# A two-layer trunk on one core: the head of the S5 gate product in two passes, the modulation columns after it, and the S5 parameters ahead of the scale

## The chip, the core and the metric

The kernel runs on one core of one Trainium2 chip. The time is device microseconds (us) of one execution. The kernel before took 1287.72 us in the median of three runs (1287.06 to 1287.97). One further execution was profiled: it took 1287.81 us, and all numbers of a trace are from it. Engines are named as the profile names them: PE does matmuls (PEld loads their weights), DVE and ACT the elementwise work, POOL is hardly used here, and SP issues nearly all DMAs.

## The reference

The input x is 512 tokens by 1024 channels, with one conditioning vector c. Two layers follow each other: an S5 state-space mixer with a gated ConvFFN, then a forgetting attention with a second ConvFFN. Every sub-layer normalizes x (RMS), multiplies by g·(1 + scale) and adds shift, where shift, scale and the gate of the residual are thirds of one product of silu(c) with a 1024x3072 matrix. The change touches the S5 mixer alone:

```
def s5_mixer(h, w_in, lam_re, lam_im, log_dt, b_re, b_im, c_re, c_im, d_skip, w_glu, w_out):
    u = h @ w_in
    ... # lb = exp(lam*dt) and k from it, per group and state
    ... # bu = (k*b) u per token;  state: hs_t = lb * hs_(t-1) + bu_t   (complex, 64 groups x 64 states)
    y = y + d_skip.astype(f32) * u.astype(f32)      # y = Re(c . hs)
    y = jax.nn.gelu(y)
    y = y * jax.nn.sigmoid(y @ w_glu.astype(f32))   # the gate product
    return (y @ w_out.astype(f32)).astype(h.dtype)
```

## The kernel before

Channels lie on the 128 partitions in KT = 8 tiles, the 512 tokens along the free side. A product of full precision is made of three matmuls per input tile k and output tile m, of 128x128 weights with 128x512 inputs: rounded weights by the rounded input (a_hi,w_hi), rounded weights by what rounding took from the input (a_lo,w_hi), and the rest of the weights by the rounded input (a_hi,w_lo). For each output tile, the 128x1024 weights come by DMA into `raw`, ACT rounds them into `w_hi` (L236), and DVE subtracts into `w_lo` (L237). `w_hi` and `w_lo` have five buffers each, `raw` three, and product sums lie in four PSUM buffers (`mmp`); smaller sums share four others (`aux`).

**The start.** After the statistics of the norm, a chain of eleven small DVE instructions makes the reciprocal root (`rms_rows`, L347 to L357), interleaved with work of the S5 parameters (`s_turn`). A product of c with the scale third (`ada_pe`, L176, which leaves rows) is turned into columns on the partitions by matmuls with a selector (L132, L137); DVE makes `ga` of it (the norm's g times 1 + scale, L142) and multiplies it into the normalized x (`a_x`, L923, eight tiles). PE then makes the first tile of u = h @ w_in (L934), with the shift third between (L176). Each output tile of u is written by ACT, sent to DRAM, and read back in another layout. The generator `s5_params` computes lb, its powers and k on DVE in small tiles; it yields y of the norm's statistics, and then runs on behind the scale.

**The loop.** Each of eight passes m over 128 channels (eight groups) makes the tables of pass m+1 (DVE and PE: L738, L747, L758, L774; ACT copies them out, L781 and L785), a triangular table `kt` that goes through DRAM and comes back as `tw`, of which ACT makes `t` (L798), an input tile m+2 (L964), and steps of the modulation products (`ada`, L176): the gate third of this mixer at m = 0 and 1, the first two thirds of the next sub-layer after that. Then comes the scan of pass m (`s5_scan`): 32 matmuls of u into the states (L813), rotation on DVE (L824 to L827), the scan itself with factors `cf` that ACT makes (L830, scan L835), and the rotation back (L842 to L845), which ends with `ua`. The outputs of pass m are summed from 16 matmuls L855 (u by t) and 32 matmuls L863 (`ua` by the table w2), ACT applies the gelu (L869, `yg`), and the result goes to DRAM and back (`s_yd`, then `yt`, in y's layout). ACT and DVE split it into `a_hi` and `a_lo` (L981, L982; `parts`), the inputs of the gate product.

**The head of the gate product.** Four output tiles of the gate product (HEAD = 4, the four `mmp` buffers) are summed input tile by input tile, as y comes in: `glu_head(k)` makes the three matmuls of each of four tiles for input tile k (L253), 96 in all. The weights of a tile are loaded and split when it is first used. ACT then makes the sigmoid (L1031, from a table that it loads first), and the other four output tiles follow as an ordinary product (L253, 96 matmuls), and the output product (192) behind it.

**What sets the order.** In the start, the order on each engine is that of the code. In the loop, a recording layer of the kernel collects the instructions and places them by dependencies and estimated costs; a note such as `issue_after(ins)` or `behind(...)` holds an instruction behind another in that order. `HEAD`, the buffers' counts and the point at which a piece of code is reached thus set where it lands. PE, DVE, ACT and SP each run their instructions in the order in which they stand, and wait there.

## Time and profile before

| | us |
|---|---|
| median of three runs | 1287.72 |
| profiled execution | 1287.81 |
| its span on the core | 1286.0 |
| PE busy in the span | 1256.1 |
| DVE busy | 773.0 |
| ACT busy | 509.3 |
| first matmul of the first tile of u (L934) | at 24.82 |
| first matmul of the last-but-one scan (L813) | at 153.09 |
| first matmul of the gate product's other tiles (L253) | at 205.30 |

Times within the trace are counted from the span's start; the profiled execution is 1.8 us longer than its span, which is what lies around it. A row of the timeline gives start, duration, engine, line, operation, output<-inputs, shapes and count, and in brackets how long the engine idled before it, with what ended that. Durations of matmul rows overlap slightly, since matmuls are pipelined; the chain of waits counts each stretch of time once. PEclk (or the column after POOL in a table of windows) is the clock that TensorE was granted, 1.00 being full speed.

### The profile page before, as it was taken

How to read it: one execution, taken by the hardware profiler on the slowest of the kernel's cores; microseconds unless marked ns; L12 is line 12 of the kernel's file. 1: busy time of each engine (PE TensorE's matmuls, PEld its weight loads, DVE VectorE, ACT ScalarE, POOL GpSimd, SP SyncE). 2: the span in 40 equal slices, each digit the busy share in tenths (PEclk: the TensorE clock that was granted, in tenths of full speed). 3: DMA queues.
4: the chain of work that ended last, by engine and by line, in shares of the span. 5: the costliest groups of instructions: out<-in, count | busy, mean ns of one | idle time of the engine just before them, and what ended most of it. 6: DMA issues, size and time to landing. Idle time of an engine off the chain costs nothing.

```text
span 1286.0 us, 17721 instructions
## 1 busy us (share of the span) xinstructions
PE 1256.1 (98%) x6822; PEld 1011.8 (79%) x6822; DVE 773.0 (60%) x1398; ACT 509.3 (40%) x929; POOL 56.9 (4%) x103
## 2 busy tenths in 40 slices
PE   7999979999999999999999999999999999999997
PEld 2566667898877878788899878778988888888887
DVE  6899866578765546665466576655754433444443
ACT  2544445335332223333333466553543322333331
POOL 0000000000000000000000343230000000000000
PEclk9999969999999999999999999999999999999999
DMA  9777665337644746644404433323143234332221
GB/s 369 236 246 234 196 227 172 99 100 244 218 151 132 237 134 200 207 133 134 150 12 131 158 124 98 128 70 95 55 131 93 68 90 127 98 99 82 68 80 67
DMA packets 73060, 183.13 MB, mean 142 GB/s; under 512 B 23079, under 2 KB 25471, under 8 KB 71951
## 3 DMA queue, kind: packets, MB, share of 16 engines
q1 hardware_dynamic: 72687, 181.46, 44.4%
q8 instruction: 54, 0.88, 0.3%
q10 hardware_dynamic: 288, 0.52, 0.1%
q14 instruction: 31, 0.25, 0.1%
HBM read 175.04 MB, written 6.92 MB: 141 GB/s over the span
## 4 chain that ended last, share of the span: by engine, by line
PE 86%; DVE 5%; ACT 5%; DMA 2%; issue 2%; SPq 0%; DVEq 0%; ACTq 0%
PE mmp L253 68%; PE mmp L964 4%; PE mmp L1106 3%; ACT s L1217 2%; PE aux L1248 2%; PE aux L774 2%; PE mmp L176 1%; DVE w_lo L237 1%; PE aux L855 1%; PE aux L863 1%; PE aux L1231 1%; ACT w_hi L236 1%; DMA raw<-in_ada_w 1%; DMA raw<-in_w_up 1%; PE aux L137 1%
## 5 line engine op out<-in xcount | busy, mean ns | idle before, releaser
L253 PE MATMUL mmp<-a_hi,w_hi 128*128 128x512 f32 (+1 forms) x944 | 361.2, 385 | 2.5 <-ACT w_hi L236 1.3
L253 PE MATMUL mmp<-a_lo,w_hi 128*128 128x512 f32 (+1 forms) x944 | 358.7, 381 | 0.0
L253 PE MATMUL mmp<-a_hi,w_lo 128*128 128x512 f32 (+1 forms) x944 | 358.6, 381 | 0.0
L236 ACT ACTIVATE w_hi<-raw 128x1024 fp32r<-128x1024 f32 (+3 forms) x201 | 194.5, 970 | 400.2 <-PE mmp L253 359.3
L237 DVE TENSOR_TENSOR w_lo<-raw,w_hi 128x1024 fp32r<-128x1024 f32 (+3 forms) x201 | 223.6, 1116 | 212.2 <-ACT w_hi L236 208.5
L253 PEld LDWEIGHTS mmp<-a_hi,w_hi 128*128 128x128 f32 x944 | 177.7, 189 | 39.2 <-ACT w_hi L236 3.2
L253 PEld LDWEIGHTS mmp<-a_hi,w_lo 128*128 128x128 f32 x944 | 178.3, 189 | 33.6
L253 PEld LDWEIGHTS mmp<-a_lo,w_hi 128*128 128x128 f32 x944 | 178.5, 189 | 31.6
L253 PE MATMUL mmp<-ghi,w_hi 128*128 128x512 f32 (+1 forms) x396 | 147.8, 373 | 0.0
L253 PE MATMUL mmp<-glo,w_hi 128*128 128x512 f32 (+1 forms) x396 | 147.2, 372 | 0.0
L253 PE MATMUL mmp<-ghi,w_lo 128*128 128x512 f32 (+1 forms) x396 | 147.1, 371 | 0.0
L319 DVE SCALAR_TENSOR_TENSOR h<-mmp,par,h 128x512 f32<-128x512 f32 (+1 forms) x56 | 37.7, 674 | 96.5 <-PE mmp L253 96.2
L253 PEld LDWEIGHTS mmp<-ghi,w_hi 128*128 128x128 f32 x396 | 74.9, 189 | 14.0
L253 PEld LDWEIGHTS mmp<-glo,w_hi 128*128 128x128 f32 x396 | 74.9, 189 | 14.0
L253 PEld LDWEIGHTS mmp<-ghi,w_lo 128*128 128x128 f32 x396 | 74.9, 189 | 14.0
L204 DVE SCALAR_TENSOR_TENSOR ada_acc<-ada_raw,sc,ada_acc 128x1024 f32<-128x1024 f32 x49 | 62.8, 1282 | 27.5 <-DMA ada_raw<-in_ada_w 27.1
L450 DVE TENSOR_TENSOR conv<-conv,mmp 128x512 f32<-128x512 f32 x44 | 30.0, 686 | 63.2 <-PE mmp L253 59.4
L446 ACT ACTIVATE conv<-conv 128x512 f32<-128x512 f32 x44 | 27.6, 632 | 101.3 <-DVE conv L443 101.3
L443 DVE SCALAR_TENSOR_TENSOR conv<-mmp,conv_wb,conv 128x511 f32<-128x511 f32 (+1 forms) x88 | 65.1, 745 | 1.9 <-ACT conv L441 0.9
L964 PE MATMUL mmp<-a_x,raw 128*128 128x512 f32 x112 | 54.7, 625 | 0.0
L253 PE MATMUL mmp<-v,w_hi 128*128 128x512 f32 (+1 forms) x160 | 43.1, 359 | 2.1 <-ACT v L236 2.1
L1217 ACT ACTIVATE s<-s,mn 128x128 f32<-128x128 f32 (+3 forms) x64 | 35.1, 550 | 10.9 <-DVE mn L1213 10.9
(240 smaller groups left out, 1570.6 us busy)
## 6 DMA issues: line engine op xcount, KB each, us to landing
raw<-in_w_up SPq DMA_DIRECT2D x88, 512.0 KB, 3.6
ada_raw<-in_ada_w SPq DMA_DIRECT2D x56, 512.0 KB, 4.4
raw<-in_ada_w SPq DMA_DIRECT2D x40, 512.0 KB, 6.6
raw<-in_w_down SPq DMA_DIRECT2D x32, 384.0 KB, 3.2
raw<-in_w_down SPq DMA_DIRECT2D x32, 320.0 KB, 3.0
nf<-nfd SPq DMA_DIRECT2D x8, 1152.0 KB, 5.9
raw<-in_fox_qk SPq DMA_DIRECT2D x16, 512.0 KB, 3.8
h<-in_x SPq DMA_DIRECT2D x8, 512.0 KB, 5.1
```

Of the source, the lines that this page charges most:

```text
L204: nc.vector.scalar_tensor_tensor(acc, w, self.sc[:, k:k + 1], acc, op0=ALU.mult, op1=ALU.add)
L236: nc.scalar.activation(hi, src, AF.Copy)
L237: nc.vector.tensor_tensor(lo, src, hi.bitcast(F32), ALU.subtract)
L253: self.last_mm = self.nc.tensor.matmul(o, wt, xt[:, cols], start=(k == 0 and n == 0), stop=(k == nk - 1 and n == 2),)
L319: self.nc.vector.scalar_tensor_tensor(self.h[:, m, cols], ps, self.par[i][:, 16 + m:17 + m], self.h[:, m, cols], op0=ALU.mult, op1=ALU.add,)
L443: nc.vector.scalar_tensor_tensor(t[:, d:], ps[:, :S - d], cw[:, 2 - d, f:f + 1], t[:, d:], op0=ALU.mult, op1=ALU.add)
L446: nc.scalar.activation(t, t, AF.Silu)
L450: nc.vector.tensor_tensor(t, t, ps, ALU.mult)
L774: nc.tensor.matmul(ps[g2][:, j, cols], x[rows, a + j, r].rearrange("p c j -> p (c j)"), self.rr[rows, planes, q, :], start=(j == 0 and r = ...
L964: nc.tensor.matmul(ps, w[m][:, k, :], x[:, k], start=(k == 0), stop=(k == KT - 1))
L1106: self.last_mm = nc.tensor.matmul(ps[q, b][:, :n], xt[:, k, tb], wt, start=(k == 0 and i == 0), stop=(k == KT - 1 and i == 2),)
L1217: nc.scalar.activation(s[:, r], s[:, r], AF.Exp, scale=-1.0, bias=mn[:, r:r + 1], accum_out=sm[:, 0, r:r + 1])
```

## The change

It has five parts.

1. **The head by passes.** `glu_head(k, part)` makes in part 0 the two matmuls with the rounded weights, in part 1 the one with `w_lo`. Part 0 runs over input tiles 0 to 6, then part 1 over 0 to 6, then input tile 7 in both parts. `w_lo` is made when part 1 first needs it, held on DVE behind the last instruction of the last scan (`self.scanned`).
2. **Loads ahead of the last scan.** The four weight tiles of the head are loaded, rounded and given their PSUM buffers at m = 7 before `s5_scan(7)` is recorded. The fourth raw tile takes a buffer of `w_lo`.
3. **Modulation columns behind the loop.** Both products of `ada` now yield before their columns; the columns of the next sub-layer's two thirds (L132, L137, `ga` L142, `par` L145) are made after the head. Those of the gate third stay at m = 1. The row that the columns read gets a buffer of its own (`ssq`).
4. **Parameters ahead of the scale.** `s5_params` yields once more before its last power step, and the part up to there is recorded ahead of the scale's columns and of `a_x`.
5. **Earlier constants.** The DMA of `s_b` and the two ACT copies that make `s_bb` of it (L606, L607) move into the loop over the first tile of u, at k = 6, ahead of the load of the second input tile's weights; `s_c` follows behind that load.

```diff
@@ ada_pe
-                rows = self.tmp.tile([P, S], F32, name="ada_rows", tag="nm_t")
+                rows = self.tmp.tile([P, S], F32, name="ada_rows", tag="ssq", bufs=1)
@@ s5_consts, s5_signs
         nc.sync.dma_start(b, self.io["s5_b"])
-        nc.sync.dma_start(self.rr[:, 5:7], self.io["s5_c"])
...
-    def s5_signs(self):
+    def s5_signs_b(self):
         nc, b = self.nc, self.s5_b
         nc.scalar.activation(self.bb[:, :, 0], b[:, :, 1], AF.Copy, scale=-1.0)
         nc.scalar.activation(self.bb[:, :, 1:3], b, AF.Copy)
+
+    def s5_signs_c(self):
+        nc = self.nc
         nc.scalar.activation(self.rr[:, 0], self.rr[:, 6], AF.Copy, scale=-1.0)
@@ s5_params
         for n in (1, 2, 4):
+            if n == 4:
+                yield
@@ s5_scan
-        nc.vector.tensor_tensor(a, a, b[:, ::-1], ALU.add)
+        self.scanned = nc.vector.tensor_tensor(a, a, b[:, ::-1], ALU.add).ins
@@ the start
                     rb = self.rms_rows(y, NB)
+                    next(params)
                     next(scale)
...
                         if k == 0:
                             load_w(0)
+                        if k == 6:
+                            self.s5_consts(keep, tp)
+                            self.s5_signs_b()
...
                     load_w(1)
-                    self.s5_consts(keep, tp)
+                    nc.sync.dma_start(self.rr[:, 5:7], self.io["s5_c"])
...
-                    behind = [self.s5_signs(), next(params), self.s5_tables(slice(0, G // 2), 0, 3), last_mm.ins]
+                    behind = [self.s5_signs_c(), next(params), self.s5_tables(slice(0, G // 2), 0, 3), last_mm.ins]
@@ the loop
-            def glu_head(k):
+            def glu_head(k, part):
+
                 for m in range(HEAD):
-                    if m not in wk:
-                        wk[m] = self.weights(self.io["s5_w_glu"][m], KT)
-                        gps[m] = self.mm.tile([P, S], F32, name="mmp")
-                    self.mms(gps[m], wk[m], (yhi, ylo), k, KT, slice(0, S))
-
-            ada = [self.ada_pe(i, (2,)), self.ada_pe(i + 1, (0, 1))]
+                    if part and m not in lo:
+                        lo[m] = self.wpool.tile([P, KT, P], F32R, name="w_lo", bufs=WB)
+                        with tc.issue_after(self.scanned):
+                            nc.vector.tensor_tensor(lo[m], raw[m], hi[m].bitcast(F32), ALU.subtract)
+                    wt = (hi, lo)[part][m][:, k]
+                    for xt in (yhi, ylo) if part == 0 else (yhi,):
+                        nc.tensor.matmul(
+                            gps[m], wt, xt[:, k], start=(k == 0 and part == 0 and xt is yhi), stop=(k == KT - 1 and part == 1)
+                        )
+
+            ada = [self.ada_pe(i, (2,), late=True), self.ada_pe(i + 1, (0, 1), late=True)]
...
-                        next(ada[m >= 2], None)
+                        next(ada[m >= 2])
+                    if m == 1:
+                        next(ada[0])
+                    if m == KT - 1:
+                        for n in range(HEAD):
+                            raw[n] = self.raw([P, KT, P], self.io["s5_w_glu"][n], 2 * (n == HEAD - 1))
+                            hi[n] = self.wpool.tile([P, KT, P], F32R, name="w_hi", bufs=WB)
+                            nc.scalar.activation(hi[n], raw[n], AF.Copy)
+                            gps[n] = self.mm.tile([P, S], F32, name="mmp")
...
             outputs(KT - 1)
-            for k in range(KT):
-                if k >= KT - 2:
+            for k in range(KT - 1):
+                if k == KT - 2:
                     parts(k)
-                glu_head(k)
+                glu_head(k, 0)
+            for k in range(KT - 1):
+                glu_head(k, 1)
+            parts(KT - 1)
+            for p in range(2):
+                glu_head(KT - 1, p)
+            next(ada[1])
```

The line numbers of the kernel after are higher from L601 on: L774 is L778 there, L813 is L817, L824 to L835 are L828 to L839, L845 is L849, L855 is L859, L863 is L867, L869 is L873, L923 is L928, L964 is L972, L981 and L982 are L989 and L990, and L1031 is L1059. The head's matmuls are at L1001 instead of L253, its `w_hi` at L1028 and its `w_lo` at L998.

The first place is DVE in the start, at the end of `rms_rows`; `s_pr`, `s_pi`, `s_kr` and `s_ki` hold the parameters, and `s_w` and `s_ring` are their scratch. Before:

```order
L705 TENSOR_SCALAR s_turn<-s_turn 128x32
L357 TENSOR_TENSOR rs_y<-rs_y,rs_t 128x4
L709 TENSOR_SCALAR s_turn<-s_turn 128x6x32
L142 SCALAR_TENSOR_TENSOR ga_99<-aux,rest 128x8
L923 SCALAR_TENSOR_TENSOR a_x<-h,ga_99,aux 128x512 x8
L509 TENSOR_TENSOR s_pr<-s_mag,s_co 128x32
```

With the change:

```order
L357 TENSOR_TENSOR rs_y<-rs_y,rs_t 128x4
L713 TENSOR_SCALAR s_turn<-s_turn 128x6x32
L509 TENSOR_TENSOR s_pr<-s_mag,s_co 128x32
L509 TENSOR_TENSOR s_pi<-s_mag,s_si 128x32
...
L680 TENSOR_TENSOR s_w_358<-s_pi,s_pr 128x64
L681 TENSOR_TENSOR s_pi<-s_w_357,s_w_358 128x2x32
L142 SCALAR_TENSOR_TENSOR ga_99<-aux,rest 128x8
L928 SCALAR_TENSOR_TENSOR a_x<-h,ga_99,aux 128x512 x8
L676 TENSOR_TENSOR s_w_357<-s_pr 128x128
```

All 27 parameter instructions ahead of the 128x128 power step now stand between the last instruction of the norm and `ga`.

The second place is PE from the last scan's matmuls (L813, now L817) on; `w` is a table, `ua` the states, of pass 6 first and of pass 7 second. Before:

```order
L813 MATMUL aux<-u,w_1528 64x64 x16
L253 MATMUL mmp<-a_hi,w_hi 128x512
L253 MATMUL mmp<-a_lo,w_hi 128x512
L863 MATMUL aux<-ua,w_1624 128x63 x16
L253 MATMUL mmp<-a_hi,w_hi 128x512
L253 MATMUL mmp<-a_lo,w_hi 128x512
L855 MATMUL aux<-u,t 128x64 x5
L137 MATMUL aux<-sel,ada_rows 128x4 x4
L855 MATMUL aux<-u,t 128x64 x3
L253 MATMUL mmp<-a_hi,w_hi 128x512
L253 MATMUL mmp<-a_lo,w_hi 128x512
L863 MATMUL aux<-ua,w_1744 128x63 x16
```

With the change (left out are only further pairs of a_hi,w_hi and a_lo,w_hi, six more before the first L867, eight and thirteen behind it and the second, four between the x28 and the x4):

```order
L176 MATMUL mmp<-raw,sc_84 32x512 x3
L817 MATMUL aux<-u,w_1528 64x64 x16
L1001 MATMUL mmp<-a_hi,w_hi 128x512
L1001 MATMUL mmp<-a_lo,w_hi 128x512
...
L867 MATMUL aux<-ua,w_1624 128x63 x16
L859 MATMUL aux<-u,t 128x64 x8
...
L867 MATMUL aux<-ua,w_1756 128x63 x16
...
L1001 MATMUL mmp<-a_hi,w_lo 128x512 x28
...
L1001 MATMUL mmp<-a_hi,w_lo 128x512 x4
L132 MATMUL aux<-rest 128x16
L137 MATMUL aux<-sel,ada_rows 128x4 x4
```

Of the head, 14 matmuls now stand ahead of the L867 of pass 6 (2 before), 16 between the two L867, behind all of L859 (4 before, with the columns' L137 and L855 among them), 26 with the rounded weights directly behind the last L867, then 28 with `w_lo`, the 12 of input tile 7, and the columns.

The third place is DVE from the last scan's rotation (L826 and L827, now L830 and L831) to the end of the head; `m` is the rotated input. Before:

```order
L826 TENSOR_TENSOR m_1726<-m_1726,m_1727 128x256
L827 TENSOR_TENSOR m_1726<-m_1726,m_1727 128x256
L142 SCALAR_TENSOR_TENSOR ga_100<-aux,rest 128x8
L835 SCALAR_TENSOR_TENSOR m_1727<-cf,m_1726 128x512
L747 TENSOR_TENSOR w_1744<-w_1744,x_1747 128x1024
L982 TENSOR_TENSOR a_lo<-yt,a_hi 128x8x64
L842 TENSOR_TENSOR ua<-m_1727,s_rot 128x512
L843 TENSOR_TENSOR ub<-m_1727,s_rot 128x256
L844 SCALAR_TENSOR_TENSOR ub<-m_1727,s_rot 128x256
L982 TENSOR_TENSOR a_lo<-yt,a_hi 128x8x64
L845 TENSOR_TENSOR ua<-ua,ub 128x512
L237 TENSOR_TENSOR w_lo<-raw,w_hi 128x1024 x3
```

With the change:

```order
L830 TENSOR_TENSOR m_1738<-m_1738,m_1739 128x256
L831 TENSOR_TENSOR m_1738<-m_1738,m_1739 128x256
L839 SCALAR_TENSOR_TENSOR m_1739<-cf,m_1738 128x512
L846 TENSOR_TENSOR ua<-m_1739,s_rot 128x512
L847 TENSOR_TENSOR ub<-m_1739,s_rot 128x256
L848 SCALAR_TENSOR_TENSOR ub<-m_1739,s_rot 128x256
L990 TENSOR_TENSOR a_lo<-yt,a_hi 128x8x64
L849 TENSOR_TENSOR ua<-ua,ub 128x512
L998 TENSOR_TENSOR w_lo<-raw,w_hi 128x1024 x4
L990 TENSOR_TENSOR a_lo<-yt,a_hi 128x8x64 x2
L237 TENSOR_TENSOR w_lo<-raw,w_hi 128x1024 x2
L142 SCALAR_TENSOR_TENSOR ga_100<-aux,rest 128x8
```

The `ga` (L142) is gone from ahead of the last scan; it stands behind the head's subtractions. Ahead of `ua`, one of the two `a_lo` and the table's product (L747, now L751) are gone as well, the latter to a place ahead of the rotation, and the four `w_lo` stand directly behind `ua`.

More of the change, by code (lines that the diff above doesn't have):

```diff
@@ L973, in s5 @@
             yhi = ylo = None
-            wk, gps = {}, {}
+            raw, hi, lo, gps = {}, {}, {}, {}
             def outputs(m):
```

## The prediction

> **What bounds the kernel now.** I read the busy line of the page first, then the table of windows over the S5 stage, then the chain of waits there, then the timeline at its end.
>
> ```profile
> PE 1256.1 (98%) x6822; PEld 1011.8 (79%) x6822; DVE 773.0 (60%) x1398; ACT 509.3 (40%) x929; POOL 56.9 (4%) x103
> 37.00:153.00 116.00, 115.82 (x924) 71.38 (x924) 103.41 (x172) 58.20 (x184) 0.00 (x0) 0.99 0.73 231
> 153.00:182.00 29.00, 22.51 (x227) 18.96 (x224) 25.89 (x37) 14.48 (x31) 0.00 (x0) 0.72 0.58 184
> 182.00:205.30 23.30, 22.50 (x91) 18.06 (x89) 5.08 (x6) 6.57 (x8) 0.00 (x0) 0.90 0.54 185
> ```
>
> PE is busy for 98% of the span, so little can be gained except where it is not busy, or busy slowly. From 37 to 153 it is full (115.82 of 116.00 us, clock 0.99). From 153 to 182 it works 22.51 of 29 us, at a clock of 0.72; from 182 on it is full again, at 0.90. The loss lies between the last scans and the head. The chain shows what set its end:
>
> ```profile
> 181.52 21.64 PE mmp L253 x84
> 203.35 1.28 ACT L1031
> 204.65 0.60 ACT nm_t L1031
> 205.30 60.48 PE mmp L253 x288
> ```
>
> From 181.52 on, 84 of the head's 96 matmuls run in one piece, then a table load and the sigmoid hold PE until 205.30, the start of the next product. What held the head back is in the timeline:
>
> ```profile
> 153.09 1.15 PE L813 MATMUL aux<-u,w 128*64 128x64 f32 x32
> 155.04 0.68 DVE L824 TENSOR_TENSOR m<-aux,s_rot 128x512 f32<-128x512 f32 x1
> 156.24 1.09 DVE L982 TENSOR_TENSOR a_lo<-yt,a_hi 128x512 fp32r<-128x512 f32 x1
> 165.52 1.05 ACT L236 ACTIVATE w_hi<-raw 128x1024 fp32r<-128x1024 f32 x1
> 166.63 0.80 PE L253 MATMUL mmp<-a_hi,w_hi 128*128 128x512 f32 x1 [1.34 <-ACT w_hi L236]
> 171.52 0.17 DVE L142 SCALAR_TENSOR_TENSOR ga<-aux,rest 128x8 f32<-128x8 f32 x1 [2.75 <-PE aux L137]
> 177.10 0.68 DVE L845 TENSOR_TENSOR ua<-ua,ub 128x512 f32<-128x512 f32 x1
> 177.84 3.68 PE L863 MATMUL aux<-ua,w 64*128 64x63 f32 x32 [4.02 <-DVE ua L845]
> ```
>
> The last sums of states (L863) start at 177.84. Of the head, only a few matmuls stand ahead of them, because weights come late (1.34 us idle before 166.63) and because the order put them behind. DVE stood 2.75 us in front of `ga` (L142), which wanted the columns' L137 on PE, all for the next sub-layer; the last scan was queued behind. PE itself then idled 4.02 us for `ua`.
>
> **The stretch with the change.** I cost PE's work from the first of the last two L813 (L817 now) to the next product at full clock, then add its waits. Prices are from the chain, where PE is full:
>
> ```profile
> 75.72 1.85 PE mmp L176 x16
> 77.57 0.32 PE aux L132 x2
> 77.89 1.08 PE aux L813 x32
> 78.97 1.93 PE aux L855 x16
> 85.25 0.79 PE aux L137 x8
> 90.19 1.93 PE aux L863 x32
> 201.62 0.39 PE L253 MATMUL mmp<-a_hi,w_hi 128*128 128x512 f32 x1
> 204.12 0.39 PE L253 MATMUL mmp<-a_hi,w_lo 128*128 128x512 f32 x1
> ```
>
> The last two rows are eleven matmuls of the head apart: 2.50/11 = 0.227 us each. By the order, the stretch holds two L817 (2 x 1.08 = 2.16), two passes of L859 (3.86), three of L867 (5.79; one is of pass 5, which stood behind this L813 before too), the last eight L176 (1.85, x16 in the trace), 96 head matmuls (21.82), and the columns L132 and L137 (1.11): 36.6 us. The same work was in the stretch before (but for one L176), so nothing is removed; what can be gained is idle time and half clock.
>
> Waits, in us after the first L817 starts. L817, half of L859, L176, L867 of pass 5, L176, the other half and the second L817 end at 7.9. The raw tile of the second `w_hi` is issued when half of the first L176 have given its buffer back, at 1.08 + 0.97 + 0.46 = 2.5; with 5.4 to the landing (below) and 1.05 for the rounding it is there at 9.0. One tile's matmuls can run till 8.3, so PE waits 0.7. Fourteen matmuls (3.2) end at 11.8, L867 of pass 6 at 13.7, L859 of pass 7 at 15.6, sixteen more at 19.3.
>
> ```profile
> raw<-in_s_w_glu SPq DMA_DIRECT2D x8, 512.0 KB, 5.4
> 190.11 1.17 DVE L982 TENSOR_TENSOR a_lo<-yt,a_hi 128x512 fp32r<-128x512 f32 x1 [4.60 <-ACT a_hi L981]
> DVE kt L786 <- ACT kt L785: 6.2, 6, 1.8
> ```
>
> The last L867 wants `ua` of pass 7. From L824 at 155.04 to the end of L845 at 177.70 were 22.7 us; without the wait for `ga` (2.75), `ga` (0.2) and four of the `a_lo` (4 x 1.09), which now stand ahead of the scan of pass 6, 15.4 remain. Begun 155.04 - 153.09 = 2.0 after the first L817, as before, `ua` is there at 17.4, ahead of 19.3. That asks that DVE reaches the scan of pass 6 in time with the four `a_lo` ahead: it stood 6.2 us in the waits for `kt`, and gets a lead in the start (below), so I count no loss; without that cover it is at most 4.4. L867 ends at 21.2, and 26 matmuls follow till 27.1, the last eight with y of pass 6. y takes 9.8 us from the end of its L863 to the end of its `a_lo` where nothing is ahead (181.52 to 191.28, pass 7): pass 6 has it at 23.5 and, behind the four `w_lo` on DVE, some 25; it is wanted at 25.3. I count 0.2. The 28 with `w_lo` last till 33.7; y of pass 7 is there at 21.2 + 9.8 = 31.0, so the twelve of pass 7 don't wait, and the second pass is what hides y's trip. They end at 36.4, the columns at 37.5. The sigmoid's way on ACT is two roundings for the next tiles, the first begun when PE has read the head's first `w_hi` for the last time, at 34.2, then the table and the sigmoid: 34.2 + 2 x 1.05 + 1.28 + 0.60 = 38.2, 0.7 beyond the columns. Sum of waits 0.7 + 0.2 + 0.7 = 1.6, stretch 38.2. Each of these meetings has under 2 us to spare and most hang on a DMA's landing; I add 1.0 for that (a fifth of one landing of 5.4), 39.2. Before, it took 205.30 - 153.09 = 52.2. **Gain 13.0.**
>
> **The start.** The moved parameters begin behind L709 instead of behind `a_x`:
>
> ```profile
> 19.33 0.26 DVE L709 TENSOR_SCALAR s_turn<-s_turn 128x192 f32<-128x192 f32 x1
> 23.82 0.17 DVE L142 SCALAR_TENSOR_TENSOR ga<-aux,rest 128x8 f32<-128x8 f32 x1 [4.23 <-PE aux L137]
> 26.12 0.43 SPq L600 DMA_DIRECT2D s_b<-in_s_b  x1
> 26.73 1.35 PE L176 MATMUL mmp<-raw,sc 128*32 128x512 f32 x8
> 29.29 0.21 DVE L509 TENSOR_TENSOR s_pr<-s_mag,s_co 128x32 f32<-128x32 f32 x1
> 34.68 0.39 DVE L674 TENSOR_TENSOR s_w<-s_pr 128x128 f32<-128x128 f32 x1
> 36.87 0.18 ACT L145 ACTIVATE par<-aux 128x8 f32<-128x8 f32 x1 [2.21 <-PE aux L137]
> 44.06 1.04 ACT L607 ACTIVATE s_bb<-s_b 128x1024 f32<-128x1024 f32 x1
> 45.14 1.23 DVE L758 TENSOR_TENSOR x<-s_lr,s_bb 128x1024 f32<-128x1024 f32 x1 [1.23 <-ACT s_bb L607]
> s_b<-in_s_b SPq DMA_DIRECT2D x1, 512.0 KB, 9.2
> ```
>
> They are 34.68 - 29.29 = 5.39 us long, and DVE had 23.82 - 19.55 = 4.27 idle there: `ga` comes 1.1 us later, `a_x` and the first L934 with it. Between L934 stand L176 that waited 0.3 for a transfer (1.35 against 1.07 for the same eight), which doesn't come later: 0.8 to 1.1 remains, and I take 0.9 as a loss of all that follows, since PE is full from there to 153. The same instructions no longer stand between `a_x` and the tables, so DVE enters the loop about 5 us ahead: the first table's x (L758, 45.14, held 1.23 by `s_bb`) can begin near 40. Nothing of that is PE time; it pays for the `a_lo` above. `s_bb` on ACT now stands ahead of the shift's `par`. Its DMA, issued at 26.12 and now one place earlier on SP's queue, lands 9.2 us later, at 35.8 if it too is 0.5 later, and the two copies (1.04 and some half of it, 1.6) end at 37.4; `par` is wanted at 36.87 + 0.9 = 37.8. Zero, and at most 1 us if the transfer is late. The load of the second tile's weights, behind `s_b` now, is issued near 26.5 and first read after 39: zero, with 5 us of cover by a landing of the size of `s_w_glu`'s.
>
> **Sum.** 1287.81 - 13.0 + 0.9 = 1275.7 for a profiled execution, which stood 0.09 above the median of the runs: **1275.6 us**. Bounds: without the allowance and half of the waits 1273.8, with something below that for later waits that shift (1272.5); with double the allowance and the late `s_bb`, 1277.7.
>
> **Rivals.** *The clock falls as before.* The last L863 took 3.68 us against 1.93 at 90.19: half clock. It fell at 166:
>
> ```profile
> 164.00:166.00 2.00, 1.28 (x24) 1.15 (x22) 1.89 (x2) 2.00 (x6) 0.00 (x0) 1.00 0.34 137
> 166.00:168.00 2.00, 1.37 (x5) 1.18 (x5) 2.00 (x4) 2.00 (x5) 0.00 (x0) 0.51 0.54 147
> 186.00:188.00 2.00, 2.00 (x9) 1.63 (x8) 0.00 (x0) 0.00 (x0) 0.00 (x0) 0.87 0.99 371
> ```
>
> At 164 to 166 PE was busy 1.28 of 2 us, still at 1.00; then 0.51, and full again only within 186 to 188 (mean 0.87, so from 186.5 on). From 177.84, when work was dense, the recovery took 8.7 us, which cost about 4.3. In my schedule the longest gap is 0.7 us, against 1.34 at 166.63, at the fall, with other idle time ahead of it. If one link is late by some 3 us (a raw tile, `t`, `ua`), PE loses the 2.8 and 4.3 behind it: 1275.6 + 7.1 = 1282.7. For it: several links have 1 us to spare. Against: 30 matmuls with rounded weights now stand ahead of the last L863, where few did. [...] I keep the rows' price.
>
> *DVE stays late.* If `ua` of pass 7 still ends near 177.8 + 0.9 (the `a_lo` find no cover, the `ga` wait is taken over by another), L867 ends at 180.6, and 66 matmuls (15.0), the columns (1.1) and 0.9 of waits lead to 197.6: 7.7 before 205.30, 1280.0. For it: DVE works 25.89 of 29 us there. Against: 2.75 us of it was a wait that is gone.
>
> *The loop turns slower.* Each pass now takes the L964 fillers behind that pass's L778, so where x comes late PE has nothing ahead of the table's matmuls. Should it wait over 2 us in each of seven passes, 14 us outweigh the gain of 12.1: 1289.6. It decides from 1.7 us a pass on. For it: DVE works 103.41 of 116 us in the loop, the wait for `kt` alone recurs in six passes. Against: DVE enters 5 us ahead, and its work per pass is unchanged and less than PE's.
>
> *The order changes nothing*, since y's trip sets the end: 1288.6 with the start's loss. Against: y of pass 7 left at 181.6 only because L863 was late.
>
> **How the numbers follow.** Forecast 0.71, the clock 0.15, DVE late 0.06, no effect 0.03, the loop 0.05. This kernel's runs differ by 0.07%, so 0.2% (2.6 us) can be told: the first three are faster, 0.92; no effect, same, 0.03; the loop, slower, 0.05. The likeliest case's own range is 1272.5 to 1277.7; the clock's and DVE's cases reach to 1283, and with both inside, about 0.2 is left out, the tails of the forecast among them.
>
> **What would show it.** The next product (L253) starts at 191 to 193 instead of 205.30; PEclk stays at 1.00 from 153 on; the last L867 takes 1.9 us and begins near 173 to 174, with under 1 us idle before it; the row of DVE's `ga` (L142) in front of the last scan is gone; 28 L1001 with `w_lo` run in one piece; the first L934 (L942) begins near 25.7; PE's windows between 40 and 150 stay above 99%. I am wrong if the loop's window shows idle PE, if the clock is at 0.5 in the head, or if the stretch is short and the time is not, which would mean that the products behind it wait for weights instead.

## The result, and the profile after

The kernel with the change takes 1281.29 us in the median (1277.81 to 1282.67, six runs) against 1287.85 us for the kernel before (1285.36 to 1290.85, six runs). The ratio is 0.9944, with a 95% interval of 0.9924 to 0.9963: 4.8 to 9.8 us faster. The profiled execution took 1280.95 us, its span is 1279.2 us. The forecast was 1275.6, so about half of the gain came.

The table of windows of the kernel after, over the same stretches (PE, PEld, DVE, ACT and POOL busy with their counts, then the granted clock, the DMA share and GB/s):

```profile
37.00:153.00 116.00, 115.58 (x873) 71.94 (x873) 96.27 (x157) 52.58 (x165) 0.00 (x0) 0.96 0.70 222
153.00:182.00 29.00, 29.00 (x288) 21.42 (x286) 27.84 (x42) 18.49 (x44) 0.00 (x0) 1.00 0.68 198
182.00:205.30 23.30, 22.58 (x115) 18.86 (x112) 12.83 (x14) 12.81 (x18) 0.00 (x0) 1.00 0.76 258
```

From 153 to 182 PE is now full at clock 1.00, where it had worked 22.51 us at 0.72. But from 37 to 153 the clock is 0.96 instead of 0.99, and the window holds 873 matmul records, not 924. It was as busy as before (115.58 us) and got less done. The chain of waits shows both halves:

```profile
24.95 0.16 DVE ga L142
37.93 1.95 PE aux L953 x16
48.55 1.95 PE aux L778 x32
74.98 2.77 PE mmp L972 x6
130.88 1.08 PE aux L817 x32
134.97 0.38 ACT w L785
135.53 1.59 PE aux L778 x8
137.12 5.42 PE mmp L972 x6
160.62 1.08 PE aux L817 x32
180.75 1.93 PE aux L867 x32
182.68 14.52 PE mmp L1001 x63
197.66 1.28 ACT L1059
198.95 0.60 ACT nm_t L1059
199.60 60.49 PE mmp L253 x288
```

The first row of the last-but-one scan (L813 before, L817 now) begins at 160.62 instead of 153.09, 7.5 us later; of this the start makes 37.93 - 37.10 = 0.83. From there to the next product it takes 39.0 us instead of 52.2. So the stretch gained 13.2 us, the start lost 0.8, and **the loop lost 6.7 us**: 122.7 us from the product of the shift (L945, now L953) to that scan, against 116.0. (The product begins 5.7 us earlier; the spans differ by 6.8, so 1.1 us more came behind it, within what two executions differ by.)

Half of the loop's loss can be read off: six L972 took 5.42 us at 137.12, and 2.77 at 74.98. Windows of the kernel after around that place (PE busy with its count, clock, DMA share, GB/s):

```profile
134.00:136.00 2.00, 1.92 (x20) 1.00 0.96 378
136.00:143.00 7.00, 7.00 (x15) 0.51 0.49 160
143.00:146.00 3.00, 3.00 (x41) 1.00 0.08 22
```

For 7 us PE worked at half clock, with hardly any idle time before it and none in it: 3.4 us lost. The remaining 3.3 us are in the table's matmuls. By line, over the loop (before from 37.05 to 153.08, after from 37.90 to 160.54), before:

```profile
L964 PE MATMUL mmp<-a_x,raw 128*128 128x512 f32 x112 | 54.7, 625 | 0.0
L774 PE MATMUL aux<-s_rr,x 64*128 64x80 f32 x256 | 22.2, 278 | 0.1
```

and after:

```profile
L972 PE MATMUL mmp<-a_x,raw 128*128 128x512 f32 x112 | 57.5, 652 | 0.0
L778 PE MATMUL aux<-s_rr,x 64*128 64x80 f32 x256 | 26.5, 282 | 0.2
```

The same 256 records take 26.5 instead of 22.2 us (under 1 us of this is the half clock, which cost the six L972 above 2.65 of its 3.4 us). One record is as long as before (282 and 278 ns), so they lie further apart: 24 of them take 3.30 us at 133.82, where 32 in one piece take 1.95 us at 48.55. Who waits for whom between 38 and 150, before and after:

```profile
ACT w L781 <- PE aux L774: 20.6, 10, 4.4
DVE x L758 <- PE aux L774: 2.0, 1, 2.0
```

```profile
ACT w L785 <- PE aux L778: 31.1, 12, 4.4
DVE x L762 <- PE aux L778: 9.6, 3, 4.9
```

ACT and DVE now wait for the table's matmuls far longer (31.1 against 20.6 us, and 9.6 against 2.0). On PE, a group in turn waits for the copies that ACT makes of earlier ones (134.97 in the chain). The chain of the kernel before has such a stop too, at 100.22, so these rows do not tell how much of the 3.3 us the stops make.

### The profile page after: what moved, and what is told of

Same layout as the page of the kernel before. It is cut to its first block, busy times and chain, and to the rows that moved or that the text cites. A ratio compares the mean times of both kernels' runs of the same rounds, so it can differ in the third digit from the quotient of the medians.

```text
span 1279.2 us, 17722 instructions
## 1 busy us (share of the span) xinstructions
PE 1256.0 (98%) x6822; PEld 1010.0 (79%) x6822; DVE 773.4 (60%) x1398; ACT 509.9 (40%) x929; POOL 56.6 (4%) x103
## 4 chain that ended last, share of the span: by engine, by line
PE 94%; DVE 3%; ACT 2%; DMA 1%; issue 1%; SPq 0%; DVEq 0%; ACTq 0%
PE mmp L253 71%; PE mmp L972 4%; PE mmp L1134 3%; PE aux L778 2%; PE mmp L1001 2%; PE aux L1276 2%; PE mmp L176 1%; PE aux L1259 1%; PE aux L867 1%; PE aux L859 1%; PE aux L1229 1%; DVE w_lo L237 1%; PE mmp L912 1%; PE aux L817 1%; PE mmp L942 1%
## 5 line engine op out<-in xcount | busy, mean ns | idle before, releaser
L253 PE MATMUL mmp<-a_hi,w_hi 128*128 128x512 f32 (+1 forms) x912 | 347.1, 382 | 1.0 <-ACT nm_t L1059 0.7
L253 PE MATMUL mmp<-a_hi,w_lo 128*128 128x512 f32 (+1 forms) x912 | 345.1, 379 | 0.0
L253 PE MATMUL mmp<-a_lo,w_hi 128*128 128x512 f32 (+1 forms) x912 | 344.9, 379 | 0.0
L236 ACT ACTIVATE w_hi<-raw 128x1024 fp32r<-128x1024 f32 (+3 forms) x197 | 190.1, 968 | 386.9 <-PE mmp L253 351.0
L237 DVE TENSOR_TENSOR w_lo<-raw,w_hi 128x1024 fp32r<-128x1024 f32 (+3 forms) x197 | 218.9, 1113 | 198.9 <-ACT w_hi L236 193.4
L253 PEld LDWEIGHTS mmp<-a_hi,w_hi 128*128 128x128 f32 x912 | 170.9, 188 | 35.8 <-issue 2.5
L253 PEld LDWEIGHTS mmp<-a_hi,w_lo 128*128 128x128 f32 x912 | 171.5, 188 | 32.2
L253 PEld LDWEIGHTS mmp<-a_lo,w_hi 128*128 128x128 f32 x912 | 171.7, 188 | 30.6
L253 PE MATMUL mmp<-ghi,w_hi 128*128 128x512 f32 (+1 forms) x396 | 147.7, 373 | 0.0
L253 PE MATMUL mmp<-glo,w_hi 128*128 128x512 f32 (+1 forms) x396 | 147.1, 371 | 0.0
L253 PE MATMUL mmp<-ghi,w_lo 128*128 128x512 f32 (+1 forms) x396 | 147.0, 371 | 0.0
L253 PEld LDWEIGHTS mmp<-glo,w_hi 128*128 128x128 f32 x396 | 74.9, 189 | 14.0
L253 PEld LDWEIGHTS mmp<-ghi,w_hi 128*128 128x128 f32 x396 | 74.8, 189 | 14.1
L253 PEld LDWEIGHTS mmp<-ghi,w_lo 128*128 128x128 f32 x396 | 74.8, 189 | 14.1
L972 PE MATMUL mmp<-a_x,raw 128*128 128x512 f32 x112 | 57.5, 652 | 0.0
L253 PE MATMUL mmp<-v,w_hi 128*128 128x512 f32 (+1 forms) x160 | 43.1, 359 | 2.1 <-ACT v L236 2.1
```

The lines of the kernel that those rows point to most:

```text
L236: nc.scalar.activation(hi, src, AF.Copy)
L237: nc.vector.tensor_tensor(lo, src, hi.bitcast(F32), ALU.subtract)
L253: self.last_mm = self.nc.tensor.matmul(o, wt, xt[:, cols], start=(k == 0 and n == 0), stop=(k == nk - 1 and n == 2),)
L972: nc.tensor.matmul(ps, w[m][:, k, :], x[:, k], start=(k == 0), stop=(k == KT - 1))
```

## The experiments

The theory after the result (A): the tail gains what was forecast; what is missing is lost in the loop, because part 5 (the earlier constants) makes the planner set the loop's matmuls in another order. Rivals: the parameters ahead of the scale (part 4) slow the loop (B), or the head's early loads do (C). Each kernel ran beside the kernel before on the same chip; ratios are to that. First the parts alone, taken out of the diff of the change as they stand there.

**Parts 1 to 3 alone**: the head by passes, its loads, and the columns.

```diff
 # as in the change: ada_pe, s5_scan, glu_head, the loop
-            ada = [self.ada_pe(i, (2,)), self.ada_pe(i + 1, (0, 1))]
+            ada = [self.ada_pe(i, (2,), late=True), self.ada_pe(i + 1, (0, 1), late=True)]
...
+                glu_head(k, 0)
+            for k in range(KT - 1):
+                glu_head(k, 1)
```

> The kernel before with parts 1 to 3 alone (head by passes, loads ahead of the last scan, columns behind the loop); the order of the loop stays as before up to the last passes. Theory A (the 6.6 us that the scan of pass 6 comes later in the profile after are made in the loop, by the new order that part 5 brings): the loop ends at 153 as before, the stretch to the next product takes 38 to 40 us, the product starts at 191 to 193, time 1274 to 1276, ratio to before 0.989 to 0.991. Rival B (the parameters ahead of the scale make the loop slower): the same as A here, parted by the two runs below. Rival C (the head's early loads and roundings hold up the loop's DMA or ACT): the loop is late here too, time about 1281, ratio 0.995.

Measured: 1275.46 us, ratio 0.9898 (0.9882 to 0.9915). Its timeline on PE, at the last-but-one scan and at the next product, and its windows:

```profile
151.97 1.15 PE L813 MATMUL aux<-u,w 128*64 128x64 f32 x32
192.45 0.50 PE L253 MATMUL mmp<-a_hi,w_hi 128*128 128x512 f32 x1 [1.35 <-ACT nm_t L1051]
120.00:153.00 33.00, 33.00 (x312) 21.56 (x310) 29.65 (x47) 14.93 (x48) 0.00 (x0) 1.00 0.72 214
153.00:182.00 29.00, 28.14 (x246) 22.18 (x242) 25.43 (x35) 15.46 (x29) 0.00 (x0) 1.00 0.66 202
```

The scan begins at 151.97, the clock is 1.00 in every window from 37 to 205, and the stretch takes 40.5 us, half a us above the expectation. C falls. This is 0.5% faster than the whole change.

**Part 5 alone**: the constants.

```diff
+                        if k == 6:
+                            self.s5_consts(keep, tp)
+                            self.s5_signs_b()
...
-                    self.s5_consts(keep, tp)
+                    nc.sync.dma_start(self.rr[:, 5:7], self.io["s5_c"])
...
-                    behind = [self.s5_signs(), next(params),
+                    behind = [self.s5_signs_c(), next(params),
```

> The kernel before with part 5 alone (s_b and its copies earlier, which also changes the recorded order of the loop: the table's matmuls stand before the input tile's). Theory A: PE reaches the scan of pass 6 some 6 to 7 us later than before (159 to 160), with table matmuls in groups of eight that wait for ACT's copies and a stretch of half clock near 136; the head in its old form does not make this up, though its order changes too: 1287 to 1295, ratio 0.999 to 1.006. Rivals B and C: the loop ends at 153 as before, ratio 0.995 to 1.001.

Measured: 1286.67 us, ratio 0.9979 (0.9963 to 0.9994), in runs from 1280.43 to 1290.26. PE's timeline:

```profile
38.67 2.61 PE L950 MATMUL aux<-par,raw 128*128 128x1 f32 x16 [0.27 <-ACT par L145]
164.30 1.15 PE L815 MATMUL aux<-u,w 128*64 128x64 f32 x32
188.96 2.00 PE L865 MATMUL aux<-ua,w 64*128 64x63 f32 x32
206.26 0.50 PE L253 MATMUL mmp<-a_hi,w_hi 128*128 128x512 f32 x1 [0.79 <-ACT nm_t L1036]
```

The loop takes 125.6 us from L950 to the scan, 9.6 more than before; it had three stretches of half clock in this execution (3.41, 3.42 and 1.71 us lost). That is A's mark. The time does not show it: it lies just below A's range and within that of B and C. The new order also puts more of the old head ahead of the last L865, the clock stays at 1.00 there, and the stretch takes 42.0 us against 52.2. So part 5 alone is even faster by 0.8 to 4.8 us; with a tail that is already good it only costs, as the runs without it show.

**Part 4 alone**: the parameters.

```diff
         for n in (1, 2, 4):
+            if n == 4:
+                yield
...
                     rb = self.rms_rows(y, NB)
+                    next(params)
```

> The kernel before with part 4 alone (parameters ahead of the scale's columns). PE's order in the loop is that of before. Theory A: only the start's delay of 0.8 to 0.9 us, 1288.6, ratio 1.0007, the scan of pass 6 at 154. Rival B: the scan of pass 6 at 159 to 160, 1294, ratio 1.005.

Measured: 1288.11 us, ratio 0.9999 (0.9989 to 1.0010), the scan at 153.36. B falls. The start's delay of 0.8 us is too small for this measurement to tell.

**Parts 1 and 2 without the columns**, shown against parts 1 to 3 alone.

```diff
-            ada = [self.ada_pe(i, (2,), late=True), self.ada_pe(i + 1, (0, 1), late=True)]
+            ada = [self.ada_pe(i, (2,)), self.ada_pe(i + 1, (0, 1))]
...
-            next(ada[1])
```

> The kernel before with parts 1 and 2 alone: the columns of the next sub-layer stay in the loop, so DVE's ga (L142) still stands ahead of some of the last scan's work. Theory A with the prediction's price of the ga wait (2.75 us): the last L863 starts up to 3 us later than with the columns behind the loop, and the clock may fall once: 1276 to 1280, ratio 0.991 to 0.994. If the columns were what held the head (rival), most of the gain is gone: 1284 to 1287, ratio 0.997 to 1.000.

Measured: 1279.07 us, ratio 0.9925 (0.9911 to 0.9939), as expected under A. Most of the gain stays without the columns, so the rival falls.

**The columns alone** (part 3 on the kernel before).

```diff
-            ada = [self.ada_pe(i, (2,)), self.ada_pe(i + 1, (0, 1))]
+            ada = [self.ada_pe(i, (2,), late=True), self.ada_pe(i + 1, (0, 1), late=True)]
...
                 glu_head(k)
+            next(ada[1])
```

> The kernel before with part 3 alone: the columns of the next sub-layer behind the head, the head in its old form. By the ga row (2.75 us waited, and the 0.2 of ga) the last L863 starts some 3 us earlier; weights of the head come as late as before, so PE still idles there and the clock may still fall: 1283 to 1285, ratio 0.996 to 0.998. With the head's form as the only thing that counts (rival): 1287 to 1288, ratio 1.000.

Measured: 1284.91 us, ratio 0.9971 (0.9958 to 0.9983). By the ratios the head is worth 9.7 us, the columns 3.7, and both 13.1, each known to about 2 us, so they add within that. The `ga` wait had been priced at 2.95. In the columns' run the clock falls in the head as before:

```profile
169.00:186.50 17.50, 14.36 (x68) 0.51 0.64 201
```

**All but the early copies.** From the whole change only the place of two ACT copies is put back; the DMA of `s_b` stays early.

```diff
                         if k == 6:
                             self.s5_consts(keep, tp)
-                            self.s5_signs_b()
...
+                    self.s5_signs_b()
                     behind = [self.s5_signs_c(), next(params),
```

> The kernel after with one thing put back: the two ACT copies of s_b stand again behind the shift of a_x, as before the change; the DMA of s_b stays early, the parameters stay ahead of the scale. The loop's recorded order on PE is then nearly that of before (input tile's matmuls ahead of the table's). Theory A (the copies' new place makes the planner reorder the loop, and that order costs the 6.6 us): the scan of pass 6 at 152 to 154, no stretch of half clock in the loop from 50 on, stretch to the next product 38 to 41, time 1274 to 1276.5, ratio 0.989 to 0.991. If the earlier DMA or the parameters were the cause: the scan of pass 6 at 158 to 161, time 1280 to 1282, ratio 0.994 to 0.996.

Measured: 1275.20 us, ratio 0.9892 (0.9875 to 0.9909). PE's timeline:

```profile
38.45 1.95 PE L952 MATMUL aux<-par,raw 128*128 128x1 f32 x16 [0.27 <-ACT par L145]
154.21 1.15 PE L817 MATMUL aux<-u,w 128*64 128x64 f32 x32
194.33 0.50 PE L253 MATMUL mmp<-a_hi,w_hi 128*128 128x512 f32 x1 [1.35 <-ACT nm_t L1059]
```

The loop takes 115.8 us again. In the six other traces with late copies and an unchanged loop (the kernel before, parts 1 to 3, part 4, parts 1 and 2, the columns, and the head without the passes below) it takes 114.6 to 118.0 us; in the two with early copies, 122.7 and 125.6. The table's matmuls take 21.8 to 22.7 us in those seven, 26.5 and 26.7 in those two, so their excess comes with the early copies and is no accident of one execution. Two ACT instructions, 1.6 us in all and never on the path, cost the change 6 us by the order that the planner makes behind them. The recorded order on PE shows how: rows of the pass in which the clock fell, from the scan's matmuls (L817) on, with the copies early (L972 is the input tile, L778 the table):

```
L817 MATMUL aux<-u,w_1066 64x64 x16
L859 MATMUL aux<-u,t 128x64 x8
L778 MATMUL aux<-s_rr,x 128x80 x12
L972 MATMUL mmp<-a_x,raw 128x512 x3
L778 MATMUL aux<-s_rr,x 128x80 x4
L867 MATMUL aux<-ua,w_1328 128x63 x16
L972 MATMUL mmp<-a_x,raw 128x512 x5
```

and with the copies back:

```
L817 MATMUL aux<-u,w_1066 64x64 x16
L859 MATMUL aux<-u,t 128x64 x8
L778 MATMUL aux<-s_rr,x 128x80 x4
L972 MATMUL mmp<-a_x,raw 128x512
L778 MATMUL aux<-s_rr,x 128x80 x4
L972 MATMUL mmp<-a_x,raw 128x512 x2
L778 MATMUL aux<-s_rr,x 128x80 x8
L972 MATMUL mmp<-a_x,raw 128x512 x2
L867 MATMUL aux<-ua,w_1328 128x63 x16
```

The wide matmuls now stand between the table's groups, where ACT's copies are waited for.

**Without the passes.** On parts 1 to 3 alone, the head goes input tile by input tile again.

```diff
-            for k in range(KT - 1):
-                glu_head(k, 0)
-            for k in range(KT - 1):
-                glu_head(k, 1)
-            parts(KT - 1)
-            for p in range(2):
-                glu_head(KT - 1, p)
+            for k in range(KT):
+                if k >= KT - 2:
+                    parts(k)
+                for p in range(2):
+                    glu_head(k, p)
```

> The version with parts 1 to 3 alone, but the head input tile by input tile with all three matmuls, as before: the second pass is taken away, the loads stay recorded ahead of the last scan. w_lo is still made behind the last scan, so only 8 of the 96 matmuls stand ahead of the last L863 (30 with the passes). If the passes carry the head's gain: the last L863 comes as early as with them, but 22 matmuls of 0.227 us more follow behind it, 5 us: 1280 to 1281, ratio 0.994, and more if PE's thin stretch before the last L863 drops the clock again (1.7 us a window). If the loads ahead carry it: 1275 to 1276.5, ratio 0.990.

Measured: 1283.84 us, ratio 0.9974 (0.9962 to 0.9986), so of the 13.1 us that parts 1 to 3 gain by their ratio, 9.8 go with the passes, and the 3.3 that are left are about what the columns gain alone. The price is above the forecast 5 us since the clock falls again. PE's timeline and a window:

```profile
167.51 2.27 PE L863 MATMUL aux<-ua,w 64*128 64x63 f32 x32 [2.22 <-DVE ua L845]
169.75 3.68 PE L855 MATMUL aux<-u,t 128*128 128x64 f32 x16
177.34 3.68 PE L863 MATMUL aux<-ua,w 64*128 64x63 f32 x32
169.00:186.50 17.50, 17.50 (x86) 0.51 0.62 191
```

The fall comes behind a wait: PE idled 2.22 us for `ua` of pass 6, and was busy for 1.78 of the 4 us from 165 to 169. From there it is busy for all 17.5 us and runs at half clock, which cost this execution 8.5 us. In parts 1 to 3 alone, twelve head matmuls run ahead of that L863 (four here), PE waits 0.45 us among them, and the clock stays at 1.00. So the passes gain mostly by what they put between the scans' small matmuls: here it filled the wait and the clock stayed.

**What drops the clock.** At the start, eight matmuls of one column (L945) run in one piece; in seven of the nine traces where these eight stand as before, the clock falls within or right behind them, between 39.0 and 41.0, and 1.7 or 3.4 us are lost. On parts 1 to 3 alone, sixteen more such matmuls were put ahead of them, and in a control four of 512 columns; neither result is used.

```diff
+                    thin = self.aux.tile([P, 1], F32, name="aux")
+                    for r in range(2):
+                        for k in range(KT):
+                            nc.tensor.matmul(thin, w[0][:, k, :], self.par[i][:, k:k + 1], ...)
 # the control:
+                    wide = self.aux.tile([P, S], F32, name="aux")
+                    for k in range(4):
+                        nc.tensor.matmul(wide, w[0][:, k + 4, :], x[:, k + 4], ...)
```

> Measures what makes the clock fall, on the version with parts 1 to 3 alone: at the start, between the columns and the product of the shift (the eight matmuls of one column, 16 in the trace, 1.95 us), sixteen more matmuls of one column are put in, 3.9 us of PE that is never idle but streams almost nothing. Their result is not used. If the clock goes by how much PE streams in a window: one to three windows at half clock follow in every run, 1.7 us lost each, so time is that of the version without plus 3.9 and 1.7 to 5.1: 1281 to 1285. If it goes by idle time alone: plus 3.9, 1279.4, and the granted clock stays 0.997.

> The control for the thin work: at the same place four matmuls of 512 columns instead (2 x 0.473 us each by the first kernel's rows, 3.8 us of PE). Their result is not used. If the clock goes by streaming: no half clock near 38 to 47, time plus 3.8, 1279 to 1280. If by idle time alone: the same, so the difference between the thin and the wide version decides: 2 to 5 us by streaming, within 1 us by idle time. The recorded order of the loop shifts a little with it, which I allow 1 us for.

Measured: thin 1282.20 us (1281.03 to 1286.33), ratio 0.9954 (0.9938 to 0.9970); wide 1278.70 us (1276.73 to 1282.16), ratio 0.9923 (0.9907 to 0.9940). The added rows take 3.6 and 3.5 us at the pace of PE:

```profile
37.39 3.73 PE L946 MATMUL aux<-par,raw 128*128 128x1 f32 x32 [0.27 <-ACT par L145]
40.98 3.52 PE L951 MATMUL aux<-par,raw 128*128 128x1 f32 x16
36.00:41.00 5.00, 4.73 (x44) 1.00 0.00 2
41.00:48.00 7.00, 7.00 (x23) 0.51 0.26 58
```

```profile
37.10 3.68 PE L945 MATMUL aux<-a_x,raw 128*128 128x512 f32 x8
40.62 1.84 PE L948 MATMUL aux<-par,raw 128*128 128x1 f32 x16
36.00:48.00 12.00, 12.00 (x48) 1.00 0.34 117
```

In the thin version PE was busy from 36 to 41 with almost no idle time, and the clock fell to half for 7 us behind it; in the wide one it stayed at 1.00. The two differ by 3.5 us in the medians, about that loss. So the clock did not go by idle time alone here.

**The product of the shift in three pieces**, on all but the early copies: two matmuls of the second input tile go between.

```diff
+                    early = self.mm.tile([P, S], F32, name="mmp")
                     for k in range(KT):
                         last_mm = nc.tensor.matmul(col, ...)
+                        if k in (1, 4):
+                            nc.tensor.matmul(early, w[1][:, k // 4, :], x[:, k // 4], start=(k == 1), stop=False)
...
-                    for k in range(KT):
+                    for k in range(2 if m == 1 else 0, KT):
```

> The run with all but the early copies, and the product of the shift (eight matmuls of one column) no longer in one piece: two matmuls of 512 columns of the second input tile stand between its second and third and its fifth and sixth. No work is added. If thin work is what drops the clock near 39 to 47: no half clock there in most runs, so 0 to 1.7 us less than the version without, 1273.5 to 1275, ratio 0.988 to 0.989; if not, the same as that version, 1275.2, ratio 0.989. The planner's order of the last passes shifts with it, which may move the time by 1 to 2 us either way.

Measured: 1281.32 us, ratio 0.9950 (0.9935 to 0.9964), a miss. The clock did not fall between 38 and 47 (it did at 26.2, for 3.4 us, ahead of the edit), but PE waited 1.59 us for the shifted x there, and the planner made another order of the last passes. In it PE waits 1.24 us for `t`, with small matmuls behind, and the clock is at half from 169.5 to 176.4:

```profile
44.95 8.85 PE L975 MATMUL mmp<-a_x,raw 128*128 128x512 f32 x20 [1.59 <-ACT a_x L963]
168.52 0.88 PE L859 MATMUL aux<-u,t 128*128 128x64 f32 x6 [1.24 <-ACT t L802]
169.33 3.53 PE L867 MATMUL aux<-ua,w 64*128 64x63 f32 x32
182.62 2.00 PE L867 MATMUL aux<-ua,w 64*128 64x63 f32 x32
```

One small edit in the start moved the last L867 by 7 us (175.80 without it), as the two copies of part 5 had done. So the time of this run does not tell what the split in the start is worth.

## Why the prediction was right and wrong

Its direction held; half of the gain did not come. 1281.29 lies outside the forecast's own range (1272.5 to 1277.7). It lies inside the wider one, which reached to 1283 for the clock's and DVE's cases in the tail, but neither of them happened: the loss was made in the loop. That it fell inside is luck.

- **The stretch** was priced at 39.2 us (36.6 of work, 1.6 of waits, 1.0 for landings) and took 39.0. The last L867 takes 1.93 us and begins 20.1 us into it (19.3 by the working), the clock is 1.00 from 153 on, `ga` is gone from ahead of the last scan. The sum fits better than its terms: PE was busy for 38.26 us, 1.7 more than priced, and idle for 0.72 instead of 2.6. Of the 1.7, 1.1 are L176, which takes 2.96 us in its three pieces (0.99, 0.98, 0.99) and was priced in one, at 1.85. PE did not wait for the second `w_hi` at all, only for the sigmoid. Where the loop was not late, it idled 2.2 and 2.0 us, for `a_lo` and the sigmoid, and the stretch took 40.5 (parts 1 to 3) and 40.1 us (all but the early copies), 1 us above the price.
- **What the stretch gained** was not told apart in the prediction. Before, PE was busy for 15.85 us at half clock between 166.00 and 186.50:

```profile
166.00:186.50 20.50, 15.85 (x72) 0.50 0.61 194
```

  Half of that, 7.9 us, is what the clock cost. Over the whole stretch PE's busy time fell from 44.92 to 38.26 us and its idle time from 7.29 to 0.72, so only half of the 13.2 us is idle time. Working at full clock from the rows covered this, but not the reason why the clock would hold.
- **The start**: 0.8 to 1.1 us were forecast, 0.83 came in the pair of traces (the shift's product at 37.93 instead of 37.10). In the four other traces whose start is unchanged the product begins between 37.20 and 38.37, so a pair of traces cannot confirm so small a term.
- **The step that failed** is the sentence in the part on the start, on DVE's lead in the loop: "Nothing of that is PE time", with the copies of `s_bb` at "Zero, and at most 1 us". The loop was priced at zero and cost 6.7 us. The rival on the loop named the right order (the table's matmuls ahead of the input tile's), with a chance of 0.05, but another wait: PE waiting for x, over 2 us a turn. It measured 6.7/7 = 1.0 us a turn, half of it clock, and PE's stop in the chain is for ACT's copies. The argument against it, that DVE enters 5 us ahead, holds (the first L762 begins at 39.58, L758 at 45.14 before) and was beside the point: it was PE that got its work in a worse order. The whole change without the two early copies takes 1275.2 us, the forecast to 0.4; since its stretch took 0.9 us more than priced, that close a fit is partly luck.
- **The rival on the clock** named the right price (7 us) and the wrong place. It looked for a link in the tail that comes late by some 3 us; no such gap was needed. In the loop after, no matmul of 512 columns stands between 130.88 and 137.12 (L817, L859, L778), PE waits for ACT for about half a us (134.97 to 135.53), and the clock falls at 136. Summed over half-microseconds from 14 to 214 us of each trace, the losses in the stretches at half clock (1 less the clock, times the time) came to 1.71, 3.4, 8.5 or 10.2 us, all multiples of 1.71 to 0.02: 1.70 and 10.24 in the kernel before, 1.71 and 3.41 after, 3.42 and 8.54 with the columns alone.
- **The indicator** "PE's windows between 40 and 150 stay above 99%" was kept (115.58 of 116.00) while the loop lost 6.7 us. The busy share showed neither the clock (0.96 against 0.99) nor a row of matmuls that is stretched by short waits inside it; the time at which the same row begins (160.62 against 153.09), or the count of matmuls in a window (873 against 924), did.

What stays open: the 3.3 us of the loop without the clock lie in the table's matmuls and come with the early copies' order. That they are waits for ACT's copies is argued from one stop in the chain, and not shown: no run tested it apart from the order.

## What to carry to other kernels

A planner's order is part of the change: an edit that is free by itself (two copies of 1.6 us) can set PE's order anew far behind it, so compare the order of the whole stage, and price where the fillers went. On a PE-bound stretch of many small matmuls, put wide ones between them, where a wait would stand above all (here the passes did so: 9.8 us by the ratios, the clock at 1.00 where it was 0.51 without them), and judge by when a given row begins and by the clock, not by the busy share. Here the version to keep is the change without the early copies (1275.20 us) or parts 1 to 3 alone (1275.46), which are the same within their intervals.

## What the runs showed of the hardware

- The clock fell with almost no idle time ahead. Behind 5 us of matmuls of one to eight columns, 4.73 us of them busy, PE ran 7 us at half clock (0.51); with 3.68 us of 512-column matmuls in the place of the added ones it ran at 1.00. In the loop of the kernel after it fell at 136.00, 5.1 us into a row of matmuls with 64 or 80 columns in which PE waited about half a us. Small matmuls alone did not always do it: in the same execution 5.6 us of them (2 to 80 columns) stand between 79.60 and 85.21, without such a wait, and the clock stayed at 1.00. The runs do not show a threshold.
- Time at half clock came in stretches of 3.4, 6.8, 17.1 or 20.5 us (twice the losses given with the rival on the clock), in eleven of the twelve traces; parts 1 to 3 alone had none between 14 and 214 us. In two kernels most of the difference between executions went with the mean clock: in the kernel after, five runs at a mean clock of 0.993 took 1280.8 to 1282.7 us, and one at 0.996 took 1277.8 (0.003 of the span is 3.8 us). With part 5 alone, twelve runs go from 1280.4 to 1290.3 us, at mean clocks between 0.997 and 0.989 (0.008 of the span is 10.3 us).
- A busy PE did not bring the clock back at once. Without the passes PE was busy for the whole of 169.00 to 186.50, at 0.51, with small matmuls and a few wide ones until 180.95; the clock was back at 186.1, 5.2 us after the work had become wide.
